# Retention keys and values loaded for two heads at once in the backward pass, rotary tables requested later, and the output projection begun inside that pass

## The chip, the cores and the metric

One core of a Trainium2 chip runs the kernel. Its engines work beside each other, each through its own list of instructions in order: TensorE (PE, matrix products), VectorE (DVE), ScalarE (ACT), GpSimd (POOL) and SyncE (SP), which here issues nearly all loads. An instruction starts when the ones before it on its engine have started and the semaphores that it waits for have come. Transfers between device memory and the on-chip memory are moved by 16 DMA engines, and an instruction on SP or ACT only requests them. The metric is the device time of one launch in microseconds (us); lower is better.

## The reference

One layer of a diffusion backbone: 2048 latent tokens in a 32x64 grid and 256 context tokens, model width 1024, float32. A normalised and modulated input goes through one projection whose columns make the parts of two groups of heads.

```
h = _modulate(_rmsnorm(x, g), scale, shift)          # context tokens as well
p = h @ w_in          # NA q,k,v,gate | RET q,k,v,gate
y_na  = neighbourhood attention(8 heads of 64)       * silu(gate)
y_ret = _rmsnorm(forward + backward retention(4 heads of 128)) * silu(gate)
out = _rmsnorm(x + ada_gate * (concat(y_na, y_ret) @ w_out))
```

The retention is what the change touches. Per head and direction it is a scan over chunks of 128 tokens with a state of 128x128, where `w_j` falls off with the distance to the chunk's end:

```
T_n = sum_j k_j^T (w_j v_j)             # one 128x128 product for a chunk
S_{n+1} = gamma^128 * S_n + T_n         # started from the state of the context tokens
o_t = sum_{s<=t} gamma^(t-s) (q_t . k_s) v_s + gamma^(t+1) q_t S
```

It is run in both directions. The first half of the output projection (columns of `y_na`) can start as soon as attention is done; the second half (`y_ret`) needs the retention.

## The kernel before, in words

Float32 products are made of three products of split operands (`hi*hi`, `hi*lo`, `lo*hi`), so that a unit of projection, 128 channels by 512 tokens or 256 tokens by 256 channels, is 24 or 48 matmuls. The program has four stages. From 0 to about 560 us the input is normalised and most columns are projected; results go to buffers in device memory (`qS`, `kS`, `rkS`, `rvS`, `rqS`, `yS`, ...). From 560 to 1017 us attention runs, window by window, with the left-over projection units woven in. From 1017 to 1091 us the **backward pass** computes the states of the scan that runs from the end. From there on the **main pass** runs forward over 16 slots (4 groups of 4 chunks, 4 heads) with the output projection woven in.

Weaving is done by `fill(n)`: it takes n steps from a generator, and each step puts 3 or 6 matmuls into TensorE's list. Until the backward pass has gone most of its way the generator makes projection units (L378 for keys and values, L367 for queries). Then `env["fill"]` becomes `out_stream()` (L1461): units of 128 tokens of the output projection, 8 steps of 3 matmuls each, which take `y` from `yS`, split it on ACT and POOL (`split_y`, L1288 and L1289) and add onto a tile `xt` of the input `x`. `plan` says how many such steps each slot of the main pass takes.

The backward pass, `back_stream()`, has 24 entries, numbered n here. n = 0 to 7 are the context tokens, four heads by two directions, with 2 chunks each. n = 8 to 23 are the latent tokens with 4 chunks each, the heads 2 and 3 alternately from the last group of chunks to the first, then heads 0 and 1. An entry needs its keys `k` and values `v` (loaded at L1172 by `load_kv`), the values weighed on ACT (`vw`, L1178), its 4 or 8 matmuls (L1184) and the recurrence on DVE (`sb`, L1214). `ahead(n)`, called at the start of entry n, requests the load of n+2 and issues the weighing of n+1. Each tile name in a pool has a number of buffers in turn (`bufs`); the request of a load into a buffer waits on SP until the readers of the buffer's last content are done. After each entry the loop takes `fill(3)`. At n = 2, 5, 8 and 11 a part of the output weights (`won`, 2 x 512 KB) is requested too.

The stores of results are delayed: `store` puts them on a list, and `tick`, called once per loop turn, issues those that are due, in this stage on ACT's queue (L151). Rotary tables for the units of retention queries are loaded by `rot_load` (L396, L399) into three buffers in turn on SP; the sine table of a unit is requested at the unit's start.

Before the change `rkS` and `rvS` hold one token per row with two heads beside each other, so one head's load has pieces of 512 bytes. After the 24 entries come `flush()`, the closing of the pools on the right side of the on-chip memory, the opening of the main pass's pools, the retention tables, `ret_tables(H)` for each head with `fill(4)` behind it, and the first loads of the main pass. In all 20 output steps run before slot 0 (`used = 20`).

A slot's normalisation goes r_c (L1371 to L1373) on TensorE, sums on ACT (L1377), a power on POOL (L1379), a scaling on ACT (L1386), then r_e (L1392) on TensorE in the next slot.

## Time and profile before

| | |
|---|---|
| median of 3 runs | 1370.25 us (1365.87 to 1372.95) |
| profiled execution | 1368.5 us, its span 1366.6 us |
| mean granted TensorE clock | 0.992 of full speed |
| TensorE busy | 1314.8 us, 96% of the span |
| VectorE, ScalarE, GpSimd busy | 60%, 44%, 43% |
| DMA mean rate | 210 GB/s over the span |

The times stand in microseconds from the span's start. A matmul counts as busy to its modelled end, so that neighbours overlap and a busy TensorE is not TensorE at its peak. TensorE is the engine that nearly always has work; what the kernel loses is found where TensorE sits idle or where its granted clock is below 1.00.

### The profile page before, as it was taken

What the parts mean: (1) busy time and instruction counts of PE and PEld (TensorE: products, weight loads), DVE (VectorE), ACT (ScalarE), POOL (GpSimd) and SP (SyncE); (2) the same over time, 40 slices, a digit from 0 to 9 for tenths busy, and PEclk for the clock granted to TensorE, in tenths of its full rate; (3) what the DMA queues carried; (4) which work ended last, traced back from release to release, by engine and by line L of the source; (5) the groups of instructions that cost most, each with busy time, mean ns of one, the idle gap of its engine ahead of it and who ended that gap; (6) DMA issues with size and microseconds to landing.
All of it is one profiled execution on the core that took longest, in us unless ns stands there. A gap on an engine that the chain in (4) does not pass through costs nothing.

```text
span 1366.6 us, 23105 instructions
## 1 busy us (share of the span) xinstructions
PE 1314.8 (96%) x8236; PEld 1151.0 (84%) x8236; DVE 825.8 (60%) x1440; ACT 607.2 (44%) x1259; POOL 587.8 (43%) x573
## 2 busy tenths in 40 slices
PE   6999999999999999999999999999999899999997
PEld 2477899887897788998999889889998789888886
DVE  5786256676665755377767777776644633345345
ACT  4454243333533344555555465556642234333332
POOL 4442201544034664345535465655422254544432
PEclk9999999999999999999999999999999999999999
DMA  9586887564867567977587787676538888555533
GB/s 310 185 275 233 281 304 186 170 205 149 323 178 230 206 210 215 268 204 204 152 225 208 209 209 235 172 209 193 147 104 281 267 263 280 166 170 170 162 120 128
DMA packets 237333, 287.25 MB, mean 210 GB/s; under 512 B 17569, under 2 KB 180513, under 8 KB 235682
## 3 DMA queue, kind: packets, MB, share of 16 engines
q1 hardware_dynamic: 204802, 228.35, 57.3%
q10 hardware_dynamic: 32416, 57.42, 11.7%
q8 instruction: 66, 1.08, 0.3%
q14 instruction: 49, 0.40, 0.1%
HBM read 194.48 MB, written 91.23 MB: 209 GB/s over the span
## 4 chain that ended last, share of the span: by engine, by line
PE 74%; DVE 8%; DMA 7%; ACT 4%; issue 3%; POOL 3%; SPq 1%; ACTq 0%; DVEq 0%; POOLq 0%
PE mm L378 20%; PE mm L675 13%; PE mm L1461 11%; PE mm L367 7%; PE sS L1021 5%; PE tr L1048 3%; PE po L1069 3%; PE mm L1184 2%; PE mm L315 2%; PE tr L1050 2%; PE po L1071 2%; DMA v<-rvS 1%; PE mm L1373 1%; PE mm L1372 1%; PE mm L1371 1%
## 5 line engine op out<-in xcount | busy, mean ns | idle before, releaser
L378 PE MATMUL mm<-whi,hlo 128*128 128x256 f32 x832 | 228.5, 282 | 0.7 <-DMA hlo<-cS 0.7
L378 PE MATMUL mm<-whi,hhi 128*128 128x256 f32 x768 | 224.3, 292 | 0.0
L378 PE MATMUL mm<-wlo,hhi 128*128 128x256 f32 x768 | 216.8, 282 | 0.0
L1052 ACT CAST pt<-tr 128x640 fp32r<-128x640 f32 (+1 forms) x128 | 95.6, 747 | 160.1 <-PE tr L1050 157.7
L1058 DVE TENSOR_TENSOR pt<-tr,pt 128x640 fp32r<-128x640 f32 (+1 forms) x128 | 113.9, 890 | 78.7 <-ACT pt L1052 77.5
L378 PEld LDWEIGHTS mm<-whi,hlo 128*128 128x128 f32 x832 | 156.1, 190 | 1.1 <-DMA hlo<-cS 1.0
L1041 POOL TENSOR_SCALAR sp<-sp,stt 128x640 f32<-128x640 f32 (+2 forms) x128 | 103.6, 812 | 106.3 <-DVE stt L1040 75.2
L378 PEld LDWEIGHTS mm<-whi,hhi 128*128 128x128 f32 x768 | 145.9, 190 | 0.0
L378 PEld LDWEIGHTS mm<-wlo,hhi 128*128 128x128 f32 x768 | 145.7, 190 | 0.0
L1030 DVE CUSTOM_DVE_ANT_0 sp<-sS,nb 128x640 f32<-128x640 f32 (+2 forms) x128 | 105.5, 825 | 34.0 <-PE sS L1021 27.7
L1035 ACT ACTIVATE sp<-sp,stt 128x640 f32<-128x640 f32 (+2 forms) x128 | 107.4, 839 | 20.5 <-DVE stt L1030 19.3
L367 PE MATMUL mm<-hhi,whi 128*128 128x512 f32 x256 | 108.1, 422 | 0.0
L367 PE MATMUL mm<-hlo,whi 128*128 128x512 f32 x256 | 101.8, 398 | 5.6 <-DVE hlo L266 2.1
L1021 PE MATMUL sS<-k,q 128*128 128x256 f32 (+3 forms) x512 | 99.1, 315 | 5.3 <-DVE stt L1030 5.1
L629 POOL TENSOR_TENSOR whi<-st,whi 128x512 fp32r<-128x512 f32 x48 | 62.9, 1332 | 95.1 <-DMA vB<-o 57.4
L367 PE MATMUL mm<-hhi,wlo 128*128 128x512 f32 x256 | 102.1, 399 | 0.3 <-DVE wlo L351 0.3
L675 PE MATMUL mm<-hhi,whi 128*128 128x512 f32 x336 | 98.2, 395 | 1.7 <-POOL whi L629 1.5
L1461 PE MATMUL mm<-wor,y 128*128 128x512 f32 x384 | 95.6, 398 | 1.9 <-DVE xt L1470 1.2
L1470 DVE TENSOR_TENSOR xt<-mm,xt 128x512 f32<-128x512 f32 x64 | 43.8, 686 | 86.1 <-PE mm L1461 86.1
L1021 PEld LDWEIGHTS sS<-k,q 128*128 128x128 f32 x512 | 82.8, 188 | 12.4 <-DVE stt L1030 8.6
L1461 PE MATMUL mm<-won,y 128*128 128x512 f32 x336 | 89.9, 406 | 0.0
L629 POOL TENSOR_TENSOR wlo<-st,wlo 128x512 fp32r<-128x512 f32 x36 | 54.0, 1501 | 76.5 <-ACT wlo L628 72.7
(258 smaller groups left out, 3065.3 us busy)
## 6 DMA issues: line engine op xcount, KB each, us to landing
st<-in_w_in_dram SPq DMA_DIRECT2D x64, 512.0 KB
q<-qS SPq DMA_DIRECT2D x64, 256.0 KB
hlo<-hS SPq DMA_DIRECT2D x20, 512.0 KB
k<-kS SPq DMA_DIRECT2D x16, 576.0 KB
kS<-o SPq DMA_DIRECT2D x16, 512.0 KB
vB<-o SPq DMA_DIRECT2D x64, 128.0 KB
qS<-o ACTq DMA_DIRECT2D x16, 512.0 KB
woS<-g ACTq DMA_DIRECT2D x32, 256.0 KB
```

The lines of the kernel that those rows point to most:

```text
L367: nc.tensor.matmul(pm[:, :n], ww[:, k, cs], h[:, k, :], start=(k == 0 and i == 0), stop=(k == KC - 1 and i == 2))
L378: nc.tensor.matmul(pm[:, t * WG:(t + 1) * WG], h[:, k, o:o + P], ww[:, k, :], start=(k == 0 and i == 0), stop=(k == KC - 1 and i == 2))
L629: nc.gpsimd.tensor_tensor(t[:, 1], r, f(t)[:, 0], ALU.subtract)
L675: nc.tensor.matmul(pm, ww[:, k, :], hh[:, k, :], start=(k == 0 and i == 0), stop=(k == KH - 1 and i == 2))
L1021: nc.tensor.matmul(o, hd["q"][i][:, hl, j * P:(j + 1) * P], k, start=(hl == 0), stop=(hl == 1))
L1030: nc.vector.tensor_tensor_reduce(T["sp"][:, :n], T["s"], nbz[big][:, o:o + n], -1.0, 3e38, ALU.add, ALU.min, T["st"][:, 0:1])
L1035: nc.scalar.activation(sp[:, :n], sp[:, :n], AF.Exp, bias=st[:, 0:1], scale=-1.0, accum_out=st[:, 1:2])
L1041: nc.gpsimd.tensor_scalar(sp[:, :n], sp[:, :n], st[:, 2:3], 0.0, ALU.mult, ALU.add)
L1052: nc.scalar.copy(pt[:, :ng_ + 2, 0, :], tr[:, :ng_ + 2, :])
L1058: nc.vector.tensor_tensor(pt[:, :n, 1, :], tr[:, :n, :], f(pt)[:, :n, 0, :], ALU.subtract)
L1461: nc.tensor.matmul(pm, yy[:, k, :], ww[:, k, sl], start=(k == 0 and i == 0), stop=(k == 3 and i == 2))
L1470: nc.vector.tensor_tensor(xts[t][:, sl], pm, xts[t][:, sl], ALU.add)
```

## The change

It has four parts. `rkS` and `rvS` are laid out by partition (token within its chunk), chunk and two heads, so that a load of both heads of a pair has rows of 4 KB and their stores have runs of 2 KB. The backward pass takes one load of `k` and one of `v` for two entries (`load_pair`), 512 KB each (256 KB for the context), with 2 buffers each; `vw` has 2 buffers in place of 3. The sine table of a rotary unit is requested at the unit's step 4 and no longer at its start. `turn()` closes the right side's pools and requests the first two `y` and `xt` behind entry 19; `out_stream` is begun at n = 21, 4 steps of it stand behind each of n = 22 and 23, 19 behind the loop, and the first seven slots of the main pass get 3 steps each (4 before).

```diff
-    rkS = [dram.tile([LT, 2 * P], F32, name=f"rkS{r}") for r in range(2)]
-    rvS = [dram.tile([LT, 2 * P], F32, name=f"rvS{r}") for r in range(2)]
+    rkS = [dram.tile([P, LT // P, 2 * P], F32, name=f"rkS{r}") for r in range(2)]
+    rvS = [dram.tile([P, LT // P, 2 * P], F32, name=f"rvS{r}") for r in range(2)]
...
                 defer(1 + r, lambda dst=dst[r], src=o[64 * r + k0:64 * r + k0 + cw]: nc.sync.dma_start(dst, src))
 
     def put_tok(dstt, c0, tp, r, n=1):
-        store(dstt[(c0 % 512) // WG][tp * 256:(tp + 1) * 256, :].rearrange("(t p) d -> p t d", p=P), r, n)
+        store(dstt[(c0 % 512) // WG][:, 2 * tp:2 * tp + 2, :], r, n)
 
     def u_rk(w, c0, tp):
         pm = yield from tokform(w, tp)
...
             n = at[0]
             at[0] += 1
             is_rq = lambda k: k >= 0 and order[k][0] is u_rq
-            if is_rq(n - 1):
-                for e in needs(n)[1:]:
-                    rot_load(*e)
             for m, v in enumerate(g):
+                if m == 4 and is_rq(n - 1):
+                    for e in needs(n)[1:]:
+                        rot_load(*e)
                 if m == 2:
                     for e in needs(n + 1)[:1 if is_rq(n) else 2]:
                         rot_load(*e)
...
         cs = slice((r % 2) * P, (r % 2) * P + P)
         res = []
         for src, nm in ((rkS, "k4"), (rvS, "v4")):
-            t = p.tile([P, 4, P], F32, name=nm, bufs=4 if nm == "v4" and p is not rt["tb"] else 3)
-            nc.sync.dma_start(t[:, :nn, :], src[r // 2][n0 * P:(n0 + nn) * P, cs].rearrange("(n p) d -> p n d", p=P))
+            t = p.tile([P, 4, P], F32, name=nm, bufs=4 if nm == "v4" else 3)
+            nc.sync.dma_start(t[:, :nn, :], src[r // 2][:, n0:n0 + nn, cs])
             res.append(t)
         return res
 
+    def load_pair(pair, n0, nn):
+        res = []
+        for src, nm in ((rkS, "k4"), (rvS, "v4")):
+            t = rt["tb"].tile([P, 4, 2 * P], F32, name=nm, bufs=2)
+            nc.sync.dma_start(t[:, :nn, :], src[pair][:, n0:n0 + nn, :])
+            res.append(t)
+        return res
+
     def weigh(p, H, v4, nn, d):
-        vw = p.tile([P, 4, P], F32, name="vw")
+        vw = p.tile([P, 4, P], F32, name="vw", bufs=2)
         nc.scalar.activation(vw[:, :nn, :], v4[:, :nn, :], AF.Copy, scale=H["w"][:, d:d + 1])
         return vw
 
...
         rp = rt["rp"]
         back = [(H, NCH, 2, d) for H in HS for d in range(2)]
         back += [(H, 4 * n4, 4, 1) for hp in (HS[2:], HS[:2]) for n4 in range(3, -1, -1) for H in hp]
-        kv, vw = {}, {}
+        kv, vw, prs_ = {}, {}, {}
 
         def ahead(n):
             if n + 2 < len(back):
                 H, n0, nn, d = back[n + 2]
-                kv[n + 2] = kv[n + 1] if n0 == NCH and d == 1 else load_kv(rt["tb"], H, n0, nn)
+                pair, hs = H["r"] // 2, slice(H["r"] % 2 * P, H["r"] % 2 * P + P)
+                if (pair, n0) not in prs_:
+                    prs_[pair, n0] = load_pair(pair, n0, nn)
+                kv[n + 2] = [t[:, :, hs] for t in prs_[pair, n0]]
             if 0 <= n + 1 < len(back):
                 H, n0, nn, d = back[n + 1]
                 vw[n + 1] = weigh(rt["tb"], H, kv[n + 1][1], nn, d)
...
     back = back_stream()
     next(back)
     fill(8)
-    for n, _ in enumerate(back):
-        tick()
-        fill(3)
-        if n == 21:
-            pre = [load_y(rt["tb"].tile([P, 4, P], F32R, name=nm), 0, t) for t, nm in enumerate(("k4", "v4"))]
-    fill(4)
-    pre = [split_y(rt["tb"].tile([P, 4, P], F32R, name="vw"), lo) for lo in pre]
-    fill(NF)
-    flush()
-    right.close()
-    env["pp"] = rt["pq"]
-...
+
+    def turn():
+        fill(NF)
+        flush()
+        right.close()
+        env["pp"] = rt["pq"]
+        rt["oy"] = pool(rp_x, "oy", 2, side="right")
+        rt["xp"] = pool(rp_x, "xp", 8, side="right")
+        rt["wr"] = pool(rp_x, "wr", 1, side="right")
+        rt["r2"] = pool(rp_x, "r2", 1, side="right")
+        rt["s2"] = pool(rp_x, "s2", 2, side="right")
+        pre.extend(load_o(0, t) for t in range(2))
+
+    xts, ready, outs, pre = {}, [], [], []
+
+    def load_xt(t):
+        xts[t] = rt["xp"].tile([P, D], F32, name="xt")
+        nc.sync.dma_start(xts[t], a["x"][t * P:(t + 1) * P, :])
+
+    def load_o(kind, t):
+        lo = load_y(rt["oy"].tile([P, 4, P], F32R, name="y1", bufs=3), kind, t)
+        if kind == 0:
+            load_xt(t)
+        return lo
+
+    def split_o(lo):
+        return split_y(rt["oy"].tile([P, 4, P], F32R, name="y0"), lo)
 
     main = [(H, n4) for n4 in range(4) for H in HS]
     J = [dict(H=H, n4=n4) for H, n4 in main]
...
             pend.pop(0)()
 
     NJ = len(J)
-    env["fill"] = out_stream()
-    for t in range(2):
-        load_xt(t)
+    for n, _ in enumerate(back):
+        tick()
+        if n < 20:
+            fill(3)
+        if n == 19:
+            turn()
+        if n == 21:
+            pre[:] = [split_o(lo) for lo in pre]
+            env["fill"] = out_stream()
+        if n > 21:
+            fill(4)
+    s2, rp, r2 = rt["s2"], rt["rp"], rt["r2"]
+    rt["wor"] = [rt["wr"].tile([P, 4, D], F32R, name=f"wor{hl}") for hl in range(2)]
+    fg = rt["wr"].tile([P, D], F32, name="fg")
+    rt["dtab"] = rt["xp"].tile([P, D], F32, name="xt")[:, :6 * P].rearrange("p (n t) -> p n t", n=6)
+    nc.sync.dma_start(rt["dtab"], a["ret_tab"])
+    rg = r2.tile([P, RH], F32, name="rg")
+    nc.sync.dma_start(rg, a["ret_g_t"])
     for H in HS:
         ret_tables(H)
         fill(4)
-    fill(1)
     tb_x.close()
     s3 = pool(ctx, "s3", 2)
     r_load(J[0])
     fill(3)
-    used = 20
+    used = 27
     q, r = divmod(48 - used, 7)
     plan = [q + (n < r) for n in range(7)] + [15] * 8 + [10] * 4
     for s in range(NJ + 3):
```

How the change moves instructions stands in the next lists: a row is the line, the operation, what it writes and reads, the shape, and the semaphores that it waits for (`DMAHW` is a transfer's end). First SP at the start of the backward pass, before: the loads of the first context entries, with the tables `rot` of the projection units between.

```order
L1172 DMA k4_10739<-rkS0_77 128x2x128 [waits DMAHW7_49,DVE_49,PE_49]
L1172 DMA v4_10741<-rvS0_79 128x2x128 [waits DMAHW1_49,DMAHW0_49,Pool_49]
L396 DMA rot_10784<-in_rot_k_dram 128x2x256
L1172 DMA k4_10812<-rkS0_77 128x2x128 [waits DMAHW2_49]
L1172 DMA v4_10814<-rvS0_79 128x2x128 [waits DMAHW4_49,DMAHW6_49,DMAHW3_49,DVE_49]
L396 DMA rot_10873<-in_rot_k_dram 128x2x256
L1172 DMA k4_10881<-rkS1_78 128x2x128 [waits DMAHW5_49]
L1172 DMA v4_10883<-rvS1_80 128x2x128
```

The same place on SP in the changed kernel:

```order
L1180 DMA k4_10739<-rkS0_77 128x512 [waits DMAHW7_49,DVE_49,PE_49]
L1180 DMA v4_10741<-rvS0_79 128x512 [waits DMAHW4_49,DMAHW1_49,DMAHW6_49,DMAHW0_49,Pool_49]
L396 DMA rot_10784<-in_rot_k_dram 128x2x256
L396 DMA rot_10869<-in_rot_k_dram 128x2x256 [waits DMAHW2_49]
L1180 DMA k4_10877<-rkS1_78 128x512 [waits DMAHW3_49]
L1180 DMA v4_10879<-rvS1_80 128x512
L1150 DMA won0_10737<-woS0_91 128x1024 [waits DMAHW5_49]
L1150 DMA won1_10738<-woS1_92 128x1024
```

The load of the first `v` covers two heads. Its tile is twice as large and its row has two more transfers to wait for, one of them the last store of attention, `yS<-y`, that ACT's queue issues at L151; before, the load of the second `v` (`v4_10814`) had that wait. The key and value load of the second head has gone from between the tables.

Next SP at the end of the backward pass, before: the loads of n = 21 to 23 and what follows them.

```order
L1172 DMA k4_11382<-rkS0_77 128x4x128 [waits DMAHW0_49,PE_49]
L1172 DMA v4_11384<-rvS0_79 128x4x128 [waits DMAHW1_49,Activation_49]
L1172 DMA k4_11405<-rkS0_77 128x4x128 [waits DMAHW2_49,PE_49]
L1172 DMA v4_11407<-rvS0_79 128x4x128 [waits DMAHW4_49,DMAHW3_49,Activation_49]
L1172 DMA k4_11420<-rkS0_77 128x4x128 [waits DMAHW5_49,PE_49]
L1172 DMA v4_11422<-rvS0_79 128x4x128 [waits DMAHW6_49,Activation_49]
L1284 DMA k4_11436<-yS0_85 128x4x128 [waits DMAHW0_49,PE_49]
L1284 DMA v4_11438<-yS0_85 128x4x128 [waits DMAHW7_49,DMAHW1_49,Activation_49]
L1319 DMA xt_11486<-in_ret_tab_dram 128x768
L1321 DMA rg_11488<-in_ret_g_t_dram 128x4 [waits DMAHW2_49]
L1400 DMA xt_11490<-in_x_dram 128x1024 [waits DMAHW3_49]
L1400 DMA xt_11492<-in_x_dram 128x1024 [waits DMAHW4_49]
```

The same place on SP in the changed kernel, from the load of the pair n = 20 and 21 on; `k4_11397` and `v4_11399` are the pair n = 22 and 23.

```order
L1180 DMA k4_11325<-rkS0_77 128x1024 [waits DMAHW6_49,DMAHW5_49,PE_49]
L1180 DMA v4_11327<-rvS0_79 128x1024 [waits DMAHW7_49,DMAHW0_49,Activation_49]
L1295 DMA y1_11389<-yS0_85 128x4x128
L1327 DMA xt_11391<-in_x_dram 128x1024 [waits DMAHW1_49]
L1295 DMA y1_11393<-yS0_85 128x4x128 [waits DMAHW2_49]
L1327 DMA xt_11395<-in_x_dram 128x1024 [waits DMAHW3_49]
L1180 DMA k4_11397<-rkS0_77 128x1024 [waits DMAHW5_49,PE_49]
L1180 DMA v4_11399<-rvS0_79 128x1024 [waits DMAHW6_49,DMAHW4_49,Activation_49]
L1295 DMA y1_11440<-yS0_85 128x4x128 [waits DMAHW7_49]
L1327 DMA xt_11442<-in_x_dram 128x1024 [waits DMAHW0_49,PE_49]
L1495 DMA xt_11481<-in_ret_tab_dram 128x768 [waits DMAHW1_49]
L1497 DMA rg_11483<-in_ret_g_t_dram 128x4 [waits DMAHW2_49]
```

Four requests of `y` and `x` (1.5 MB) stand ahead of the last pair, and the last pair waits on PE for entry n = 19, whose buffer it takes. Behind these rows the fourth `y` (`y1_11496`) waits on PE for the first output unit, the fifth waits for the second unit and has the loads of slot 0 behind it, and the sixth waits for the third unit and has those of slots 1 and 2 behind it.

Last TensorE at the end of the pass in the changed kernel (L1192 is L1184 of before): the first row is n = 19, `k4_11325` is n = 20 and 21 in one row, `k4_11397` is n = 22.

```order
L1192 MATMUL mm<-vw,k_11274 128x128 x4
L367 MATMUL mm<-hhi,whi 128x512
L367 MATMUL mm<-hlo,whi 128x512
L367 MATMUL mm<-hhi,wlo 128x512
L1192 MATMUL mm<-vw,k_11325 128x128 x8
L1192 MATMUL mm<-vw,k_11397 128x128 x4
L1461 MATMUL mm<-won_10737,y_11423 128x512
L1461 MATMUL mm<-won_10737,y_11389 128x512
L1461 MATMUL mm<-won_10738,y_11423 128x512
```

Before, n = 20 to 23 stand there one behind the other, and the first L1461 comes after n = 23. Now the four steps of output stand between n = 22 and n = 23.

## Rows read from the trace of the kernel before

**Rows 1.** Chain of waits, 990 to 1115 us: start us, us, what.

```profile
1042.22 5.32 DMA k<-rkS
...
1081.12 0.89 PE mm L1184 x8
...
1082.02 0.70 PE mm L367 x3
...
1084.09 4.76 DMA v<-rvS
...
1088.95 0.73 ACT vw L1178
```

**Rows 2.** TensorE in time, entries: start, us, line, operation, count, [idle before <-releaser].

```profile
1023.51 0.60 PE L1184 MATMUL mm<-vw,k 128*128 128x128 f32 x4
...
1049.19 1.16 PE L1184 MATMUL mm<-vw,k 128*128 128x128 f32 x8 [1.69 <-ACT vw L1178]
...
1055.89 1.16 PE L1184 MATMUL mm<-vw,k 128*128 128x128 f32 x8 [0.49 <-ACT vw L1178]
...
1074.90 1.16 PE L1184 MATMUL mm<-vw,k 128*128 128x128 f32 x8 [0.78 <-ACT vw L1178]
...
1080.96 1.05 PE L1184 MATMUL mm<-vw,k 128*128 128x128 f32 x8
...
1084.02 1.16 PE L1184 MATMUL mm<-vw,k 128*128 128x128 f32 x8 [0.41 <-ACT vw L1178]
...
1086.70 1.16 PE L1184 MATMUL mm<-vw,k 128*128 128x128 f32 x8 [1.53 <-DVE sb L1214]
...
1089.72 2.08 PE L1184 MATMUL mm<-vw,k 128*128 128x128 f32 x8 [1.86 <-ACT vw L1178]
```

**Rows 3.** SP and ACT in time, start of the backward pass.

```profile
1019.98 0.37 SPq L1172 DMA_DIRECT2D v<-rvS  x1
...
1022.61 0.36 SPq L1172 DMA_DIRECT2D v<-rvS  x1
...
1019.99 0.46 ACTq L151 DMA_DIRECT2D yS<-y  x1
...
1022.62 0.51 ACT L1178 ACTIVATE vw<-v,w 128x256 f32<-128x256 f32 x1 [5.02 <-DMA yS<-y]
```

**Rows 4.** Stretches: PE, PEld, DVE, ACT, POOL busy (count), granted clock, DMA share, GB/s.

```profile
78.00:82.00 4.00, 4.00 (x12) 3.17 (x11) 4.00 (x4) 1.54 (x2) 3.92 (x3) 0.57 1.05 370
...
102.00:104.00 2.00, 0.56 (x3) 0.47 (x3) 2.00 (x3) 0.00 (x0) 1.44 (x1) 1.00 0.43 138
...
1026.00:1036.00 10.00, 10.00 (x87) 10.00 (x86) 4.89 (x16) 2.69 (x7) 6.20 (x8) 1.00 1.04 360
...
1084.00:1086.00 2.00, 1.16 (x8) 0.97 (x8) 1.92 (x5) 0.07 (x1) 0.19 (x1) 1.00 0.90 259
...
1090.00:1096.00 6.00, 6.00 (x20) 5.16 (x21) 1.04 (x3) 3.70 (x11) 4.90 (x8) 0.57 1.05 383
```

**Rows 5.** SP in time, a rotary sine table of the backward pass.

```profile
1041.78 0.35 SPq L399 DMA_DIRECT2D rot<-in_rot_s_dram  x1
```

**Rows 6.** ACT and POOL in time, splitting of the first `y`.

```profile
1089.70 0.62 ACT L1288 CAST vw<-k 128x512 fp32r<-128x512 f32 x1
...
1090.39 1.27 POOL L1289 TENSOR_TENSOR k<-k,vw 128x512 fp32r<-128x512 f32 x1 [3.32 <-ACT vw L1288]
```

**Rows 7.** TensorE and ACT in time, one slot of the main pass.

```profile
1130.18 0.39 PE L1373 MATMUL mm<-sfs,qs 128*128 128x128 f32 x2
...
1134.72 0.60 PE L1392 MATMUL mm<-ident,rjk 128*128 128x128 f32 x4
...
1133.17 1.14 ACT L1386 ACTIVATE rjk<-mm,rss 128x128 f32<-128x128 f32 x4 [1.42 <-POOL rss L1379]
```

**Rows 8.** SP and TensorE in time, slot 1 of the main pass.

```profile
1099.71 0.50 SPq L1172 DMA_DIRECT2D k<-rkS  x1
...
1110.28 0.60 PE L1336 MATMUL mm<-ident,k 128*128 128x128 f32 x4
```

More of the change, by code (lines that the diff above doesn't have):

```diff
@@ L1298, in hybrid_kernel @@
     fill(8)
-    for n, _ in enumerate(back):
-        tick()
-        fill(3)
-        if n == 21:
-            pre = [load_y(rt["tb"].tile([P, 4, P], F32R, name=nm), 0, t) for t, nm in enumerate(("k4", "v4"))]
-    fill(4)
-    pre = [split_y(rt["tb"].tile([P, 4, P], F32R, name="vw"), lo) for lo in pre]
-    fill(NF)
-    flush()
-    right.close()
-    env["pp"] = rt["pq"]
-    oy = pool(rp_x, "oy", 2, side="right")
-    xp = pool(rp_x, "xp", 8, side="right")
-    wr_ = pool(rp_x, "wr", 1, side="right")
-    r2 = rt["r2"] = pool(rp_x, "r2", 1, side="right")
-    s2 = pool(rp_x, "s2", 2, side="right")
-    rp = rt["rp"]
-    rt["wor"] = [wr_.tile([P, 4, D], F32R, name=f"wor{hl}") for hl in range(2)]
-    fg = wr_.tile([P, D], F32, name="fg")
-    rt["dtab"] = xp.tile([P, D], F32, name="xt")[:, :6 * P].rearrange("p (n t) -> p n t", n=6)
-    nc.sync.dma_start(rt["dtab"], a["ret_tab"])
-    rg = r2.tile([P, RH], F32, name="rg")
-    nc.sync.dma_start(rg, a["ret_g_t"])
+    def turn():
[20 more added lines that the diff above has]
+        return split_y(rt["oy"].tile([P, 4, P], F32R, name="y0"), lo)
     main = [(H, n4) for n4 in range(4) for H in HS]
@@ L1394, in r_e @@
         y_put(4 + r, n4 // 2, (n4 % 2) * 512, gg)
-    xts, ready, outs = {}, [], []
-    def load_xt(t):
-        xts[t] = xp.tile([P, D], F32, name="xt")
-        nc.sync.dma_start(xts[t], a["x"][t * P:(t + 1) * P, :])
-    def load_o(kind, t):
-        lo = load_y(oy.tile([P, 4, P], F32R, name="y1", bufs=3), kind, t)
-        if kind == 0:
-            load_xt(t)
-        return lo
-    def split_o(lo):
-        return split_y(oy.tile([P, 4, P], F32R, name="y0"), lo)
     sqo = {}
@@ L1479, in hybrid_kernel @@
     NJ = len(J)
-    env["fill"] = out_stream()
-    for t in range(2):
-        load_xt(t)
+    for n, _ in enumerate(back):
[16 more added lines that the diff above has]
+    nc.sync.dma_start(rg, a["ret_g_t"])
     for H in HS:
```

## The prediction

> **What bounds the kernel now.** I began with the table of busy time: TensorE is busy for 96% of the span, so only its idle time and its slow clock can be won back. The chain of waits between 990 and 1115 us shows where that time lies: it is TensorE's own work up to 1042 us, and from there on transfers of keys or values stand in it ahead of entries of the backward pass, each about 5 us long; two of them are in [rows 1]. Behind the last entry the chain is TensorE again, with the output projection.
>
> TensorE in time gives the price [rows 2]. An entry of 0.89 us and three steps of 0.70 [rows 1] make 2.99 us from one entry to the next when nothing is late. From entry 9 (1049.19) to entry 19 (1080.96) are 31.8 us, where ten such distances are 29.9: 1.9 us are lost at entries 11 and 17, which wait 0.49 and 0.78 us for a weighed `v` and start slowly. Entry 9 itself waits 1.69 us. Together that is 3.6 us. At the end of the pass, where the projection units have run out, n = 21, 22 and 23 wait 0.41, 1.53 and 1.86 us, 3.8 in all.
>
> Third, the stretches [rows 4]. Behind these last gaps TensorE is busy throughout 1090 to 1096 us at a granted clock of 0.57, most of it at 1.2 GHz in place of 2.4; the same work at 1.00 needs 0.43 x 6 = 2.6 us less. All that the change can win in this pass is 3.6 + 3.8 + 2.6 = 10 us, 0.7% of the kernel.
>
> Why are the entries late? Loads with rows of 4 KB moved 360 GB/s in 1026 to 1036 us; with pieces of 512 bytes of keys and values, 1084 to 1086 moved 259 [rows 4]. And SP stood at the request of a sine table until 1041.78 us, with the next keys right behind it, at 1042.22 [rows 5, 1].
>
> **The change part by part, against the profiled execution.** Its time is 1368.5 us, 1.9 above its span and 1.75 below the median shown. The sum is carried from 1368.5; the median lies inside the range.
>
> *Pairs in the middle of the pass.* Half as many requests, rows of 4 KB. The pair for n = 8 and 9 now stands ahead of the sine table that held SP, and the data of n = 11 and 17 are requested with those of n = 10 and 16. At 360 GB/s a pair (1.05 MB) takes 2.9 us, and two entries take 6.0, so a pair requested when entry n-3 ends is there before n. I take all 3.6 us as won; bounds 0 (at n = 8 and 11 another 1.05 MB of `won` lie between, and with two buffers no request can go earlier) and 3.6. The later sine tables are worth at most a part of the same stalls and have no term of their own. The runs of 2 KB in the stores cost nothing: they go out on ACT's queue, for which TensorE waits nowhere in this pass but at its start, and that is the next term.
>
> *The start of the pass.* Before, the first `v` was requested at 1019.98 and the second at 1022.61, when the last store of attention, issued at 1019.99 on ACT's queue, had landed; weighing began at 1022.62 and the first entry at 1023.51, with no idle time [rows 3, 2]. The first `v` is now for both heads, lies over that store's source too, and waits for it. So it is requested at 1022.61, 2.6 us later. Weighing followed 2.6 us behind the request, and the entry 0.9 behind weighing: 1026.1 in place of 1023.5, 2.6 us idle, since nothing stands between on TensorE's list. Behind the wait on SP are the next two rotary tables and the second pair, which is needed some 10 us later. Bounds: 0, if the store lands early; 4.3, if the clock falls too, as in 78 to 82 us (0.57 over 4.0 us busy: 1.7 lost). It need not: 102 to 104 us has 1.44 us idle at 1.00 [rows 4]. I take 2.6.
>
> *The end of the pass.* Entry 19, at 1080.96 before, comes at 1080.96 - 3.6 + 2.6 = 1080.0, and n = 21 ends 3.4 us later (three entries of 0.89, a step of 0.70), at 1083.4. The pair for n = 20 is requested when n = 17 is done, at 1074.9. Behind it on SP follow two `y` and two `xt`, then the pair for n = 22, which waits for entry 19. From 1074.9 on the DMA engines have to move two pairs (2.1 MB), `y` and `xt` (1.6 MB) and three stores of rotated queries (0.8 MB), 4.46 MB: 12.4 us at 360 GB/s. So the last pair lands at 1087.3, and n = 22 runs behind its weighing of 0.73 us [rows 1], at 1088.1. TensorE is idle for 4.7 us; the projection steps are used up and the output steps stand behind n = 22. The splitting of the first `y` sits on ACT behind that weighing: 0.73 + 0.62 on ACT and 1.27 on POOL [rows 6] end at 1089.9, 0.9 us past the end of n = 22. Idle 5.6 in place of 3.8: +1.8. Bounds: at 259 GB/s the pair lands 4.8 us later, +6.6; if it finds the queues free when entry 19 ends (1080.9 + 2.9 + 0.8 = 1084.6), idle is 1.2 and the term -2.6.
>
> The Trainium skill, in "Perfetto Trace Analysis", DMA Optimizations, speaks on both sides: its first rule is that larger transfers use the memory better, its second that smaller ones may let some start sooner where the DMA engines are generally idle. By the second, the last pair in halves would let n = 22 start 1.5 us sooner (0.52 MB at 360 GB/s), and one load for two entries costs that; by the first the term stays at +1.8. The trace is on the side of the first: the DMA share is 0.90 in 1084 to 1086 us and 1.05 in 1090 to 1096 [rows 4], so the engines are not idle.
>
> *The clock behind it.* The gap is longer than before, so the fall in 1090 to 1096 us stays: 0 as its change, between -2.6 (no fall) and +1.7.
>
> *Output steps moved from the main pass to before it.* All 48 steps of 0.7 us are done by the end of slot 6, as before. But in the slot shown the chain from r_c over ACT and POOL ends at 1134.31 with ACT's scaling, and r_e follows at 1134.72 [rows 7]: 0.4 us of slack. One step less between r_c, whose last matmuls start at 1130.18, and r_e leaves it waiting 0.3 to 0.4 us in the four slots s = 3 to 6: +1.4. Bounds 0 and 2.8 (a whole step each).
>
> *Loads for the first slots.* SP now waits for output units 0 and 1 before it can request the keys of slot 0, and for unit 2 before those of slots 1 and 2. Before, slot 1's keys were requested at 1099.71 and used at 1110.28 [rows 8]. Unit 2 ends with the 24th of 27 steps ahead of slot 0, so they are now requested 2.1 us ahead of it, and slot 1's first matmul comes 0.4 + 3 x 0.7 = 2.5 behind slot 0's: 4.6 us in all, where the transfers in the chain took 4.8 to 5.3 [rows 1]. I take +0.5; bounds 0 and 3 (slot 2's loads stand behind).
>
> **Sum.** -3.6 + 2.6 + 1.8 + 0 + 1.4 + 0.5 = +2.7 us: 1371.2 us. What the pairs win in the middle is paid at both ends.
>
> **Rivals.** *A, faster: the last pair is not late.* If `y` and `xt` have drained by the end of entry 19, the end term is -2.6, the clock does not fall (-2.6) and r_e has its slack: -3.6 + 2.6 - 2.6 - 2.6 + 0.5 = -5.7, 1362.8 us. For it: the 2.6 MB ahead of the pair need 7.3 us at 360 GB/s, from 1074.9 to 1082.2. Against it: the stores, `y`'s own pieces of 512 bytes, and 259 GB/s in 1084 to 1086.
>
> *B, slower: the DMA engines decide at the end.* If the mixture of pairs, `y`, `xt` and stores drains at 259 GB/s, n = 22 comes 4.8 us later, and if the clock falls at the start as well (1.7) the sum is 2.7 + 4.8 + 1.7 = +9.2, 1377.7 us. It decides from about 300 GB/s downwards (4.46 MB then take 14.9 us, 2.5 more than in the sum). For it: the 259 and the 512-byte pieces of `y`; against it: the rows of 4 KB in all the rest.
>
> *C, the change doesn't do what it says.* With two buffers each pair waits for the entry three before it, and `won` fills the stretch behind n = 8 and 11, so that the stalls in the middle come back as waits for a pair: 3.6 us more, 1374.8 us. Against it are 6.0 us for 2.9 us of transfer.
>
> **How the numbers follow.** My forecast, with its small errors, has 0.50 (1367 to 1376 us by itself), A 0.20, B 0.17, C 0.13. About 0.5%, 6.9 us, is what a measurement of this kernel can tell from no change: under 1363.4 or over 1377.1 us. A lies just past that line and with its spread counts for 0.15 faster, the forecast's lower edge for 0.03: 0.18. B counts for 0.13 slower, C and the forecast's upper edge for 0.05: 0.18. Same is the rest, 0.64. The range, 1363 to 1378.5, reaches to the centres of A and B.
>
> **What would show it.** Right: the first entry has about 2.6 us idle, with a `v` requested at 1022.6; n = 9, 11 and 17 have none; n = 22 has 4 to 6, released by the weighing of a `v` that landed at about 1087; r_e in slots 3 to 6 has some 0.3 each. Wrong: under 2 us idle at n = 22 (A), over 8 (B), idle time at every second entry released by a pair (C), or a main pass whose slots of 3 steps are bound by another engine, which no term here prices.

## The result, and the profile after

The changed kernel takes 1373.41 us in the median of 22 runs (1370.70 to 1381.82), the kernel before 1367.64 us in 22 runs (1364.93 to 1373.63): a ratio of 1.0044 (95% interval 1.0032 to 1.0055), 6 us slower. That is inside 1363 to 1378.5 us and within 0.5% by its middle value. Against the profiled execution of before the forecast was +2.7 us; the changed kernel's profiled execution has a span of 1371.1 us, 4.5 more.

TensorE in time, the entries of the backward pass in the changed kernel (L1192 is L1184 of before), answers to [rows 2]:

```profile
1025.97 0.71 PE L1192 MATMUL mm<-vw,k 128*128 128x128 f32 x4 [1.93 <-ACT vw L1186]
...
1050.02 1.05 PE L1192 MATMUL mm<-vw,k 128*128 128x128 f32 x8
...
1055.97 1.05 PE L1192 MATMUL mm<-vw,k 128*128 128x128 f32 x8
...
1074.07 1.05 PE L1192 MATMUL mm<-vw,k 128*128 128x128 f32 x8
...
1080.02 1.05 PE L1192 MATMUL mm<-vw,k 128*128 128x128 f32 x8
...
1081.61 1.05 PE L1192 MATMUL mm<-vw,k 128*128 128x128 f32 x8
...
1087.36 3.90 PE L1192 MATMUL mm<-vw,k 128*128 128x128 f32 x16 [4.70 <-ACT vw L1186]
```

The first entry has 1.93 us idle where it had none. The request of the first `v` stood on SP until attention's last store, issued at 1020.36, had landed:

```profile
1022.66 0.34 SPq L1180 DMA_DIRECT2D v<-rvS  x1
```

The forecast had 1022.6 for it and 1026.1 for the entry, which came at 1025.97; the idle time is shorter than 2.6 us because TensorE came to the entry 0.5 us later than before (1024.04). Entries 9, 11 and 17 (the second, third and fourth row) have none where they had 1.69, 0.49 and 0.78. Entry 19 stands at 1080.02; 1080.0 was forecast. Then n = 20 runs at 1081.61, and the idle time of 4.70 us, the size that was forecast, lies one entry earlier than forecast: the row at 1087.36 is n = 21 and n = 22 together. ACT in time at that place:

```profile
1080.57 0.72 ACT L1186 ACTIVATE vw<-v,w 128x512 f32<-128x512 f32 x1 [4.12 <-DMA v<-rvS]
...
1086.16 0.33 ACTq L151 DMA_DIRECT2D rqS<-o  x1
...
1086.59 0.72 ACT L1186 ACTIVATE vw<-v,w 128x512 f32<-128x512 f32 x1 [5.29 <-POOL o L409]
...
1088.79 0.72 ACT L1186 ACTIVATE vw<-v,w 128x512 f32<-128x512 f32 x1 [1.48 <-DMA v<-rvS]
```

Weighing for n = 21 (1086.59) did not wait for data; its pair had been used for n = 20 at 1080.57. It stood behind the request of a store, issued at 1086.16, that waits for POOL to finish the last rotated queries (L409). `turn()` issues the last stores behind entry 19, ahead of that weighing. The chain of waits shows what would have held the next entry in any case:

```profile
1077.30 6.50 DMA rqS<-o
...
1083.87 4.81 DMA v<-rvS
...
1088.79 0.73 ACT vw L1186
...
1089.56 1.70 PE mm L1192 x8
```

The last `v` was requested at 1083.87, 2.8 us behind its `k`. Its request waits for an earlier store of rotated queries, which was moving from 1077.30 to 1083.80, among `y`, `xt` and the pair. `v` landed at 1088.68 and n = 22 ran at 1089.56. But the held request is little of that. Its `k`, requested at 1081.10 and not held, landed only at 1086.94 by the trace's landing events, and `v` came 1.74 us behind it. In the profile of e3 below the request of the last `v` is not held, and it lands 1.33 us behind its `k` (1083.67 to 1085.00); in that of e1 it is held for 3.2 us and lands 1.31 behind (1082.97 to 1084.28). So the held request is worth some 0.4 us here, as an estimate from these differences; the rest is what stood ahead of the pair in the DMA engines, as was forecast. The waits of SP's queue in 1075 to 1090 us name the wait of the held request (us in total, times, longest):

```profile
SPq L1180 <- DMA rqS<-o: 2.4, 1, 2.4
```

Stretches of the same place (columns as in [rows 4]):

```profile
1078.00:1088.00 10.00, 5.30 (x32) 4.59 (x32) 6.15 (x15) 1.44 (x2) 1.26 (x1) 0.97 1.04 376
...
1088.00:1090.00 2.00, 1.88 (x9) 1.58 (x9) 0.49 (x2) 1.21 (x3) 0.00 (x0) 0.50 1.02 379
...
1090.00:1092.00 2.00, 2.00 (x11) 1.67 (x11) 1.56 (x5) 1.16 (x3) 1.90 (x2) 0.82 0.57 206
```

The DMA engines moved 376 GB/s in 1078 to 1088 us, at a busy share of 1.04, where before 259 were moved at the pass's end [rows 4]. The rate was the forecast's 360 and not the 259 of rival B, and the engines had no pause. The Trainium skill, "Perfetto Trace Analysis", DMA Optimizations, says in its first rule that larger transfers use the memory better; the trace agrees, by these two numbers. The clock fell behind the gap, to 0.50 in 1088 to 1090 us, and was 0.82 in the mean of the next 2 us: in this execution a shorter fall than before.

Further on, in the main pass, five places of TensorE in time (L1351 is a slot's first line, L1407 is r_e, the last two rows are the output projection):

```profile
1114.45 0.65 PE L1351 MATMUL mm<-ident,k 128*128 128x128 f32 x4 [0.59 <-DMA k<-rkS]
...
1126.16 0.63 PE L1351 MATMUL mm<-ident,k 128*128 128x128 f32 x4 [0.18 <-DMA k<-rkS]
...
1137.24 0.65 PE L1407 MATMUL mm<-ident,rjk 128*128 128x128 f32 x4
...
1152.24 1.10 PE L1407 MATMUL mm<-ident,rjk 128*128 128x128 f32 x4
...
1166.62 0.50 PE L1461 MATMUL mm<-wor,y 128*128 128x512 f32 x1 [1.64 <-ACT y L1299]
...
1167.97 4.00 PE L1461 MATMUL mm<-wor,y 128*128 128x512 f32 x11 [0.85 <-POOL y L1300]
```

Slot 1 waits 0.59 and slot 3 waits 0.18 us for keys, as [rows 8] let expect. r_e takes 0.60, 0.65 and 0.64 us in slots 3 to 5, where it took 0.60 before, so it hardly waits there; in slot 6 it is stretched to 1.10. ACT's scaling ahead of r_e in slot 4:

```profile
1136.38 1.14 ACT L1401 ACTIVATE rjk<-mm,rss 128x128 f32<-128x128 f32 x4 [1.42 <-POOL rss L1394]
```

It ends at 1137.52, and r_e starts at 1137.24: r_e's first product needs only the first of the four scaled parts. In slot 6 the power on POOL begins at 1150.78, because two products for the slot's queries (L1362, 2.51 us from 1147.91) stand ahead of it there.

The two last rows of TensorE I had not foreseen: at 1166.62 and 1167.97 the first unit of the second half of the output projection, which needs the fourth head's `y` of the first group, waits 1.64 + 0.85 us. Its chain, first in the changed kernel, then before:

```profile
1156.84 6.12 DMA yS<-rgg
...
1162.97 2.96 DMA y<-yS
...
1165.95 0.63 ACT y L1299
...
1166.64 1.28 POOL y L1300
```

```profile
1155.07 4.72 DMA yS<-rgg
...
1159.81 2.99 DMA y<-yS
```

The store `yS<-rgg` is issued 1.8 us later and takes 6.1 us in place of 4.7; the load behind it takes the same time. Of the 1.8 us, 1.06 are the lateness of the whole slot (slot 7 begins at 1156.55, before at 1155.49). Against the slot's first matmul the store is 0.7 us later: 0.28 us behind it, before 0.42 ahead of it. The store stands on ACT behind the sums of r_c (L1392). With three steps a slot none is left behind r_c, which so ends right at the slot's end, one step of 0.7 us later against the next slot. Before, this unit waited 0.70 us (1164.84). The clock fell behind the stall, to 0.50 in 1170 to 1172 us; before it was 1.00 there.

Times between marks sum this up. The marks are the first matmul of n = 0 (the idle time ahead of it stands in the first column), of n = 19, and of slots 0, 7 and 8. Where 27 steps run ahead of slot 0, 7 x 0.695 = 4.87 us are taken from the third column and added to the fourth, so that all rows hold the same work. From slot 8 to the end all lie between 194.1 and 194.7 us. A row is one execution, and some lie far from their kernel's median: that of e1 4.5 us under it, p1 3.4 and j1 3.2 under, e2 2.0 over. So the table says where time lies, and the medians say how much the kernels differ.

| one profile each | idle, n = 0 | to n = 19 | to slot 0 | to slot 7 | to slot 8 | sum | ratio of times |
|---|---|---|---|---|---|---|---|
| before | 0 | 57.45 | 26.07 | 48.46 | 16.73 | 148.7 | 1 |
| changed | 1.93 | 54.05 | 26.28 | 50.25 | 20.41 | 152.9 | 1.0044 |
| changed, again | 1.93 | 55.68 | 27.41 | 51.27 | 17.30 | 153.6 | |
| p1 pairs alone | 1.90 | 54.17 | 24.80 | 48.45 | 15.77 | 145.1 | 0.9981 |
| p3 p1, old tables | 2.01 | 55.76 | 25.96 | 48.45 | 15.78 | 148.0 | 0.9996 |
| p2 early output alone | 0 | 57.67 | 29.66 | 51.00 | 17.13 | 155.5 | 1.0066 |
| e1 start mended | 0 | 53.83 | 27.61 | 50.45 | 17.05 | 148.9 | 1.0021 |
| e2 store at once | 1.98 | 55.92 | 25.78 | 51.46 | 16.27 | 151.4 | 1.0032 |
| e3 turn behind n = 20 | 1.99 | 54.63 | 26.16 | 51.21 | 17.28 | 151.3 | 1.0028 |
| j1 slot loads early | 1.85 | 54.56 | 26.77 | 50.24 | 16.97 | 150.4 | 1.0033 |
| c1 p1, start mended | 0 | 54.65 | 25.13 | 48.46 | 16.83 | 145.1 | 0.9981 |
| c2 c1, store at once | 0 | 54.12 | 24.78 | 48.45 | 15.77 | 143.1 | 0.9968 |
| c3 all four mended | 0 | 53.98 | 24.75 | 49.20 | 16.38 | 144.3 | 0.9988 |

By this table the change gives 3.4 us in the middle of the pass and takes 1.9 at its start, 0.2 at its end, 1.8 in slots 0 to 6 and 3.7 behind them, in this one execution.

### The profile page after: what moved, and what is told of

The parts are those of the page before. It is cut to its first block, busy times and chain, and to the rows that moved or that the text cites. A ratio compares the mean times of both kernels' runs of the same rounds, so it can differ in the third digit from the quotient of the medians.

```text
span 1371.1 us, 23050 instructions
## 1 busy us (share of the span) xinstructions
PE 1315.0 (96%) x8236; PEld 1151.4 (84%) x8236; DVE 827.3 (60%) x1440; ACT 606.3 (44%) x1259; POOL 587.6 (43%) x573
## 4 chain that ended last, share of the span: by engine, by line
PE 41%; DMA 10%; DVE 7%; POOL 5%; issue 5%; ACT 4%; SPq 1%; ACTq 1%; POOLq 0%; DVEq 0%
PE mm L1461 10%; PE mm L378 10%; PE sS L1021 4%; PE tr L1048 3%; PE po L1069 3%; PE mm L367 2%; DMA woS<-g 2%; PE mm L1192 2%; PE tr L1050 2%; PE po L1071 1%; DMA k<-rkS 1%; DMA vB<-o 1%; POOL g L763 1%; PE mm L1387 1%; PE mm L1386 1%
## 5 line engine op out<-in xcount | busy, mean ns | idle before, releaser
L1461 PE MATMUL mm<-won,y 128*128 128x512 f32 x384 | 100.5, 404 | 0.0
L1461 PE MATMUL mm<-wor,y 128*128 128x512 f32 x384 | 96.9, 401 | 3.5 <-ACT y L1299 1.6
L1461 PEld LDWEIGHTS mm<-wor,y 128*128 128x128 f32 x384 | 70.5, 190 | 20.2 <-issue 3.5
```

The costliest lines, as they stand in the source:

```text
L1461: nc.tensor.matmul(pm, yy[:, k, :], ww[:, k, sl], start=(k == 0 and i == 0), stop=(k == 3 and i == 2))
```

## Experiments

Times are medians; ratios are against runs of the kernel before on the same chip, with 95% intervals. Differences between two changed kernels are differences of their ratios, since not all ran on one chip.

**p1, the pairs alone.** The kernel before with `load_pair`, the new layout and the later tables; its loop and its output are those of before.

```
     for n, _ in enumerate(back):        # as before: fill(3) after every entry,
         tick()                          # y requested at n = 21,
         fill(3)                         # 20 output steps between the passes
...
```

> The kernel before with the pair loads, the new layout and the later sine tables, but the output projection begun where it was (20 steps between the passes). Ledger theory: the middle of the backward pass gives -3.6 us, its start costs +2.1 (first v behind the store of attention), and the end gains, since the last pair is requested when n = 19 is done with nothing queued ahead of it: first output step at about 1088.5 instead of 1091.5, so in all 3 to 5 us under before, some 1363 to 1365 us. Rival: the early output is not what costs, the last pair comes late with or without it; then the end stays as before and the kernel is within 1.5 us of before (1366 to 1368).

Measured: 1365.19 us, 0.9981 (0.9968 to 0.9993). Faster than before, by 2.6 us; less than was expected. TensorE in time:

```profile
1022.49 0.71 PE L1192 MATMUL mm<-vw,k 128*128 128x128 f32 x4 [1.90 <-ACT vw L1186]
...
1076.66 1.05 PE L1192 MATMUL mm<-vw,k 128*128 128x128 f32 x8
...
1083.67 3.58 PE L1192 MATMUL mm<-vw,k 128*128 128x128 f32 x16 [3.48 <-ACT vw L1186]
...
1087.01 0.48 PE L1472 MATMUL mm<-won,vw 128*128 128x512 f32 x1
```

The middle and the start are as in the changed kernel. At the end n = 22 still waits 3.48 us, though only its own pair is asked for: the pair has to wait for entry 19's buffer. The first output unit is at 1087 us, 10.4 us behind entry 19 (1076.66); before it was 10.5 (1080.96 to 1091.45). So by the end of the entries the pairs have neither gained nor lost anything there; the 1.3 us that the table shows as gain to slot 0 (26.07 to 24.80) come behind that, where the clock was already back at 1.00. Stretches of the same place:

```profile
1083.00:1087.00 4.00, 3.33 (x16) 3.33 (x17) 2.13 (x7) 1.85 (x3) 0.47 (x1) 0.57 0.96 294
...
1087.00:1093.00 6.00, 5.64 (x27) 4.43 (x26) 1.74 (x4) 4.13 (x13) 5.43 (x10) 1.00 1.07 381
```

The clock fell behind the 3.48 us of idle time here too, but under the last two entries (0.57 in 1083 to 1087 us), and the output units run at 1.00; before, 1090 to 1096 us had 0.57 [rows 4].

**p2, the early output alone.** The changed kernel with the loads, the layout and the table requests of before.

```
...
-                    prs_[pair, n0] = load_pair(pair, n0, nn)
...
+                kv[n + 2] = kv[n + 1] if n0 == NCH and d == 1 else load_kv(rt["tb"], H, n0, nn)
...
```

> The kernel before with the early output alone (loads of one head in pieces of 512 bytes, sine tables as before). Ledger: the last pass entries wait behind y and xt (about +2 to +4 us with 512-byte pieces), the slots lose 2, the first unit of the second half 1.5: 1372 to 1375 us. Rival: the early output costs only together with the pairs, whose loads of 1 MB it has to stand in line with: 1368 to 1370.

Measured: 1376.23 us in 6 runs, 1.0066 (1.0043 to 1.0089). The two parts add up: 0.9981 and 1.0066 make 1.0047, the whole is 1.0044. All of the loss is the early output's. TensorE in time, and stretches:

```profile
1089.38 2.08 PE L1184 MATMUL mm<-vw,k 128*128 128x128 f32 x8 [4.75 <-ACT vw L1178]
...
1093.14 2.07 PE L1184 MATMUL mm<-vw,k 128*128 128x128 f32 x8 [1.68 <-ACT vw L1178]
```

```profile
1088.00:1096.00 8.00, 4.94 (x19) 4.45 (x20) 2.20 (x7) 3.20 (x5) 2.43 (x3) 0.52 1.11 336
```

The same 4.75 us ahead of n = 21 as in the changed kernel, 1.68 more ahead of n = 22, and a low clock for 8 us: 29.66 us to slot 0 in place of 26.07.

**e1, the start.** The first context tiles are allocated with the two chunks that they hold. The tile with four reached into the source of attention's last store, by the waits in the order of instructions; how far, no run shows.

```
-            t = rt["tb"].tile([P, 4, 2 * P], F32, name=nm, bufs=2)
+            t = rt["tb"].tile([P, nn, 2 * P], F32, name=nm, bufs=2)
```

> The changed kernel with the first context tiles allocated at the size they use (2 chunks), so that the first v no longer lies over the source of attention's last store. If the wait on that store is the price of the start, v is requested near 1020.4 us instead of 1022.7, the first entry has no idle time and the kernel is about 2 us faster than the changed one (1371.4). Rival: the 2 us come back as idle time at the end of the pass, where transfers set the time: 1373.

Measured: 1370.95 us, 1.0021 (1.0007 to 1.0035), under the changed kernel's 1.0044 with intervals that just overlap. The request of the first `v`, and TensorE in time:

```profile
1017.96 0.34 SPq L1180 DMA_DIRECT2D v<-rvS  x1
```

```profile
1021.54 0.71 PE L1192 MATMUL mm<-vw,k 128*128 128x128 f32 x4
...
1082.74 2.07 PE L1192 MATMUL mm<-vw,k 128*128 128x128 f32 x8 [4.74 <-ACT vw L1186]
...
1085.15 2.08 PE L1192 MATMUL mm<-vw,k 128*128 128x128 f32 x8 [0.34 <-ACT vw L1186]
```

The first `v` is requested while attention's last store is only being issued (1017.97), and the first entry's idle time is gone. The 4.74 us ahead of n = 21 are as long as they were, so nothing of it was given back there; in this profile the low clock behind them costs 1.3 us more (27.61 to slot 0), as in the second profile of the changed kernel (27.41).

**e2, the store of `y`.** Issued right behind r_e in slots 6, 10, 14 and 18.

```
         fill(part[2])
+        if s >= 6 and s % 4 == 2:
+            flush()
         if 0 <= s - 2 < NJ:
```

> The changed kernel, but the store of the fourth head's y is issued on ACT's queue right behind its computation in slots 6, 10, 14 and 18 and no longer at the next slot's start, where it stands behind r_c's sums. If the first unit of the second half of the output projection is late because that store is (1156.84 us, 1.8 later than before, landing 3.2 later), it is issued near 1154 us, the 2.5 us idle and the low clock behind them go, and the kernel is 3.5 us faster than the changed one (1370). Rival: the load of y is held by the transfers of the next slot, not by the store's issue: under 1 us faster.

Measured: 1371.66 us, 1.0032 (1.0019 to 1.0045): 1.6 us under the changed kernel, not clear of it by the intervals, and half of what was expected. TensorE in time at the first unit of the second half:

```profile
1169.59 0.48 PE L1461 MATMUL mm<-wor,y 128*128 128x512 f32 x1
...
1170.29 2.79 PE L1461 MATMUL mm<-wor,y 128*128 128x512 f32 x11 [0.21 <-POOL y L1300]
```

0.21 us idle in place of 2.49. The stall was the store's, but its size in the first profile was an extreme: see the next run.

**The changed kernel again.**

> The changed kernel once more, for a second profile. The first unit of the second half of the output projection was 3.7 us late in the first profile, 0.3 to 0.6 us in two variants with the same order there. If that stall belongs to the order (the store 1.8 us later), the idle time is there again, over 2 us; if it hangs on how the transfers fall in one execution, it is under 1 us.

Measured: one run, 1372.90 us. The first unit of the second half waits 0.85 us, 17.30 us from slot 7 to slot 8. By the line drawn ahead of it, under 1 us, the 2.49 us hang on how the transfers fell in the first execution. What stays with the order is small: the unit waits 0.84 to 0.86 us in the profiles of p2, e1, e3 and j1 too, and in four with the order of before 0.70, 0, 0 and 0.80 (before, p1, p3, c1). From slot 7 to slot 8 that is 17.0 to 17.3 us against 15.8 to 16.8, some 0.9 us in the mean. This execution lost its time elsewhere. Stretches at the start of its pass:

```profile
1026.00:1028.00 2.00, 2.00 (x12) 2.00 (x11) 0.64 (x2) 2.00 (x7) 1.90 (x3) 0.52 0.91 286
...
1028.00:1030.00 2.00, 2.00 (x13) 2.00 (x13) 1.42 (x4) 0.93 (x3) 2.00 (x4) 0.62 0.94 306
```

Behind the idle time of the first entry the clock fell to 0.52 and 0.62, so that entry 1 came 4.15 us behind entry 0 in place of 2.6 to 2.7: 1.5 us. The clock fell there in the profiles of e2 (entry 1 after 3.72 us) and p3 (4.20) too, and not in those of p1, e3, j1 and the first of the changed kernel, all with 1.9 to 2.0 us idle.

**e3, turn one entry later.**

```
-        if n == 19:
+        if n == 20:
             turn()
```

> The changed kernel with the closing of the pools and the first requests of y and x one entry later, behind n = 20: the last pair stands ahead of y and x on SP, and the last store of rotated queries behind the weighing of n = 21 on ACT. If these two waits are the price of the end, n = 21 has no idle time, the last pair lands near 1084.5, n = 22 runs at about 1087 instead of 1089.6 and the kernel is 2 us faster than the changed one. Rival: y, which comes behind the pair now, is split too late and the first output unit waits instead: no gain.

Measured: 1371.02 us, 1.0028 (1.0015 to 1.0041), 2.2 us under the changed kernel, with intervals that overlap. TensorE, ACT and stretches:

```profile
1081.05 2.05 PE L1192 MATMUL mm<-vw,k 128*128 128x128 f32 x16 [0.34 <-ACT vw L1186]
...
1086.33 2.08 PE L1192 MATMUL mm<-vw,k 128*128 128x128 f32 x8 [3.23 <-ACT vw L1186]
```

```profile
1085.10 0.33 ACTq L151 DMA_DIRECT2D rqS<-o  x1
...
1085.55 0.72 ACT L1186 ACTIVATE vw<-v,w 128x512 f32<-128x512 f32 x1 [3.94 <-POOL o L409]
```

```profile
1086.00:1092.00 6.00, 5.67 (x17) 4.85 (x18) 1.50 (x5) 2.02 (x4) 2.55 (x2) 0.50 1.04 374
```

Both waits moved as expected: n = 20 and 21 (the first row) wait 0.34, n = 22 runs 7.4 us behind entry 19 in place of 9.5. But its weighing (1085.55) now stands behind the same store that waits for POOL, 0.5 us behind the landing of its `v` (1085.00), and the clock behind the gap stays at 0.50 for 6 us. To slot 0 the table shows 0.1 us won on the first profile of the changed kernel and 1.3 on the second. The first output unit does not wait, so the rival's reason is not seen either. That the two waits priced the end is therefore not shown: what was won in idle time went to the clock in part, and the medians leave 2.2 us that are not clear of noise.

**j1, slot loads ahead of the fourth `y`.**

```
     nc.sync.dma_start(rg, a["ret_g_t"])
+    for X in J[:2]:
+        r_kv(X)                         # keys and values of slots 0 and 1
...
```

> The changed kernel, but keys and values of slots 0 and 1 are requested right behind the last pass entry, ahead of the fourth y and its wait for the first output unit. If the late keys of slot 1 are what slots 0 to 3 lose (1.1 us in the profile, 1.7 to 2.3 in three others), slot 1 has no idle time and the kernel is 1 to 2 us faster than the changed one. Rival: the transfer of slot 1's keys is long in any case and idle time only moves to slot 2: no gain.

Measured: 1371.03 us, 1.0033 (1.0016 to 1.0051): not told apart from the changed kernel. TensorE in time:

```profile
1112.03 0.60 PE L1356 MATMUL mm<-ident,k 128*128 128x128 f32 x4
...
1124.47 0.63 PE L1356 MATMUL mm<-ident,k 128*128 128x128 f32 x4 [0.95 <-DMA k<-rkS]
```

Slot 1 starts without idle time, and slot 3 waits 0.95 us: the wait moved on, as the rival had it. 50.24 us to slot 7, as in the first profile of the changed kernel (50.25); the second has 51.27.

**p3, the pairs with the old table requests.**

```
+            if is_rq(n - 1):
+                for e in needs(n)[1:]:
+                    rot_load(*e)
             for m, v in enumerate(g):
-                if m == 4 and is_rq(n - 1):
...
```

> The pairs alone, with the sine tables requested at the unit's start as in the kernel before. If the later request is worth nothing (the sine table that SP waits for longest is requested in the unit before and isn't moved), this is as fast as the pairs alone: 1365 us, within 1 us. Rival: the later request frees SP for the pair loads; without it entries of the pass wait 2 to 4 us in all: 1368.

Measured: 1366.14 us, 0.9996 (0.9981 to 1.0011), against 0.9981 (0.9968 to 0.9993) of the pairs alone: not told apart. In its profile no entry from 8 to 19 has idle time, so SP was in time for the pairs without the later request; the 2.9 us by which its sum is longer are a low clock behind the first entry (4.2 us to the second) and 1.2 us at the end. The later request has shown no worth.

**c1 and c2, the pairs with mended start, and with the store at once.** The edits of e1 and e2 on p1.

> The pairs alone (output projection begun as before), with the first context tiles at the size they use. If the pairs' gain in the middle and at the end of the pass and the price of the start add up, this is 2 us under the pairs alone, near 1363 us. Rival: the start's 1.9 us are hidden by a wait at the end of the pass (n = 22 waits for transfers in any case): 1365.

> As the one before, and the fourth head's y stored right behind its computation. In the kernel before and with the pairs alone the first unit of the second half waits 0 to 1.2 us, so this gives 0 to 1 us more: 1362 to 1363. Rival: an earlier store blocks ACT's queue in front of r_c's sums: no gain or 1 us loss.

Measured: c1 1364.10 us, 0.9981 (0.9966 to 0.9996), c2 1363.71 us, 0.9968 (0.9955 to 0.9982). The start's idle time is gone from both profiles, but c1 is not faster than p1 by its ratio. The reason given for the rival, a longer wait of n = 22, holds for little: it waits 3.78 us in place of 3.48, and in c1's profile another 1.1 us lie between slots 7 and 8. c2 is the fastest kernel here, 4 us under before and 10 under the changed one.

**c3, the early output with all waits treated.** The edits of e1, e2, e3 and j1 together.

> The early output kept, with all its waits treated: first context tiles at their size, turn behind n = 20, the fourth head's y stored at once, keys and values of slots 0 and 1 requested ahead of the fourth y. If the waits named are the whole price of the early output, it comes to 2 + 2 + 1.7 + 1 us under the changed kernel, 1366 to 1367 us, level with before, and still 3 us behind the pairs alone with their start mended; since TensorE has the same work, an early output can win nothing that the pairs have not won. Rival: begun early and unhindered it wins back the idle time at the end of the pass, and is at 1363 or less.

Measured: 1365.29 us, 0.9988 (0.9973 to 1.0003). Some 8 us under the changed kernel, level with before, and no better than the pairs alone. TensorE in time, n = 22:

```profile
1084.10 2.08 PE L1192 MATMUL mm<-vw,k 128*128 128x128 f32 x8 [3.86 <-ACT vw L1186]
```

n = 22 still waits 3.86 us. The early output steps stand behind n = 22, so they cannot fill that time; the sum to slot 0 (24.75) is that of c2 (24.78).

## Why the prediction came out right, point by point

- **Pairs in the middle: -3.6 forecast, -3.4 measured** (57.45 to 54.05), -3.3 with the pairs alone. No wait for a pair came back (rival C is out), and two buffers sufficed.
- **The start: +2.6 forecast, 1.9 idle measured** in every kernel that has the tile of four chunks; e1 took it away. The mechanism and the time of the first entry were right; the size was 0.7 too large, since TensorE reached the entry later. The bound with a falling clock was real: three of seven profiles with this idle time show it, at 1.0 to 1.5 us.
- **The end: +1.8 forecast, +0.2 and +1.3 in the two profiles.** The last pair came late as forecast, behind `y`, `xt` and the stores in the DMA engines: it landed at 1088.68 and n = 22 ran at 1089.56, where 1087.3 and 1088.1 were forecast. What the forecast had not is a second wait inside the same time: a store on ACT that waits for POOL, ahead of the weighing of n = 21. It shows as the idle time of 4.70 us; that this equals the forecast's 4.7 is luck, since that was for n = 22 and for another releaser. The splitting of `y` did not hold TensorE. The low clock was shorter than before in the first profile; in the second, with the same 4.70 us, it was 0.50 from 1088 to 1094 us, and there the 1.1 us between the two lie. The DMA rate of rival B (259) did not come: 376.
- **r_e and the slots' loads: +1.4 and +0.5 forecast, +1.8 together measured**, in other shares: 1.1 by slot 3 (late keys), 0.7 behind it. Four more profiles with the same loads (the second one, e1, e2, e3) have 2.0 to 3.0. The term for r_e was too large: 0.3 to 0.4 us in each of four slots were forecast, and slots 3 to 5 have 0 to 0.05, slot 6 has 0.5. The forecast measured the slack to the end of ACT's scaling, but r_e begins when the first of its four parts is done; and slot 6 waits for POOL, which the term did not price. That the two terms together come out near their sum is luck in part.
- **The step that was missed** is the sentence that all 48 steps are done by the end of slot 6, as before, from which only r_e's chain was drawn. The steps hid more than that chain: with no step behind r_c the store on ACT behind r_c's sums is issued 0.7 us later against the next slot. The stretch from slot 7 to slot 8, with the first unit that needs that store, is 3.7 and 0.6 us longer in the two profiles than before. The larger of the two is one execution's; e2 puts the price in the median at about 1.6 us, not clear of zero, and the profiles without that execution at some 0.9.
- **The sum**: +2.7 forecast, 6 measured: the median lies within the small errors stated for the forecast (1367 to 1376), on the side of what it did not have. The two profiles of the changed kernel show 4.2 and 4.9 by the table, and what lacks in the forecast is the late `y` in the first, the falling clock at the start and more lateness in the slots in the second. Most of the rest of the 6 us is that the profiled execution of before was 0.9 us above its median and those of the changed kernel 0.4 and 0.5 under theirs. Rival A's -5.7 did not come; the pairs without the early output gave 2.6 (p1) to 4.4 us (c2), and the last entry but one waits 3.5 to 3.9 us there as well.

Not settled: what the end would cost without the store on ACT, since in e3, where it holds n = 22 by 0.5 us only, the clock took part of what was won. That the last store could be kept out of ACT's way was not tried. Nor do the runs part the pairs' gain in the middle into its possible causes, rows of 4 KB and requests one entry earlier.

## What to carry to other kernels

Filling work put early is worth only what it fills: here it stood behind the entry that waited, and taken from the slots it laid bare a chain that it had hidden there. Slack ahead of an instruction that takes its input in parts counts from the first part. When a tile grows, look which older buffer it now touches: here that tied the first load to a store. And an order change that closes a stage early issues that stage's last stores early too, on a queue where others stand behind them.

## What the runs showed of the hardware

A request for a load can wait for the landing of a store to which no data tie it: the last `v` was requested at 1083.87, 2.8 us behind its `k`, because it takes up a completion semaphore last used by a store that landed at 1083.80 (eight take turns in this program, each waited for before it is used again). A request held so need not cost its time: with the DMA engines at a busy share of 1.04, this `v` landed 1.74 us behind its `k`, where 1.33 were seen without the wait (e3). And idle time of 1.9 to 2.0 us ahead of the first entry let the clock fall to about 0.5 in three of seven profiles and not in the others.
